# Neighbouring weight slabs of an expert kernel: one transfer of 8 KB rows for two of 4 KB

## The chip, the cores and the metric

The kernel runs on one core of one Trainium2 chip. The metric is device time in microseconds (us) of one execution. Engines are named as in the profile: PE (matrix multiply), DVE (vector), ACT (scalar), POOL (GpSimd), SP (the engine that issues most transfers). A transfer is carried out by 16 DMA engines that all queues share.

## The reference, cut to what matters

One block of a transformer: a projection, two attention branches with gates, an output projection with residual, and then a mixture of experts. The change lies in the last. Every token is weighted over its two chosen experts of 32:

```python
    weights = pg_sel * pe_top / jnp.sum(pe_top, axis=-1, keepdims=True)
    global_idx = g_idx * EXPERTS_PER_GROUP + e_idx
    combine = jnp.sum(jax.nn.one_hot(global_idx, N_EXPERTS, dtype=jnp.float32) * weights[..., None], axis=1)
    out = jnp.zeros((n, d), jnp.float32)
    for e in range(N_EXPERTS):
        hidden = jax.nn.silu(t @ w_gate[e]) * (t @ w_up[e])
        out = out + combine[:, e:e + 1] * (hidden @ w_down[e]).astype(jnp.float32)
```

There are 1024 tokens of 1024 values and 256 hidden values per expert; everything is float32.

## The kernel before, in words

The stages ahead of the experts (projection, attention, gates, output projection, router) take about 900 us of the span. The output projection runs over eight blocks of 128 tokens (`out_mm`, `x2_half`, `route`); weights for the experts are prefetched beside it.

**Weights.** The three matrices of an expert are laid out as one array `w_exp` of 128 partitions and 6144 values, and are read in six slabs of 128 x 1024 values, 512 KB each, 4 KB to a partition: 192 slabs for 32 experts, always in the same order (`raw_order`). A slab lands in a raw buffer. `weights(e, j0, j1)` then splits it into a high and a low part (`split`: ACT copies, rounding, L83; DVE subtracts, L84), and when that is done its buffer is free. Raw buffers come in units: five `er` and four `ex` (`N_RAW`, `N_MORE`) hold one slab each, and eight `ring` buffers hold two, side by side in a partition. When all slabs of a unit have been split, `weights` calls `load` for the next slabs in the order. `load_pairs` takes a new ring buffer. In `load`, each slab has a transfer of its own, on SP's queue. At the start 9 single slabs and 8 pairs are loaded; the pairs one after the other, as the output projection frees their buffers. As pairs are split in the expert stage, the first of them are not loaded again while at least `R_RAW` = 13 slabs are loaded or on their way: their buffers go to the gathers (`gbuf`, up to 9) and, after that, to the finished blocks (`ybuf`).

**One expert.** POOL gathers up to 112 rows of `h2_d` by token number (`gather`, L1111). PE transposes them (`tokens`, L1119), multiplies them with gate and up (`gate_up`), transposes the hidden values (`hidden_t`) and multiplies with down (`down`); each product is three matmuls (`mm3`, L87 to L89). In `down`, ACT writes the first half of the block, scaled by the tokens' weights, into a y buffer (L1160), DVE the second (L1162). POOL then scatters the block into `out`, adding to what is there (L1163). Scatters write the same array, so each waits for the one before it to have landed. A y buffer is used again when its scatter has landed.

**Order.** For PE, DVE and ACT the order around the router is that of the code; elsewhere a scheduler sets it at build time, from the code's order and from when buffers come free. SP's and POOL's queues run strictly in order. A transfer on SP's queue counts its landing in one of eight counters, taken in turn, and waits for the transfer that used the counter before it.

Of the kernel before, what the change touches and what calls it, by code (L numbers as in the profile page):

```python
# [10 lines left out]
F32 = mybir.dt.float32  # L11
# [13 lines left out]
P = 128  # L25
# [10 lines left out]
XTB = 4  # L36
NGB = 3
NYB = 3
N_MORE = 4
GB = 9  # L40
R_RAW = 13
LAGO = 1
# [6 lines left out]
def kernel(ctx: ExitStack, tc: tile.TileContext, a, out):  # L49
    nc = tc.nc  # L50
    left = dict(side="left", reuse_waits="tile")
# [30 lines left out]
    def split(hi, lo, src, eng=None):  # L82
        nc.scalar.activation(hi, src, AF.Copy)  # L83
        return (eng or nc.vector).tensor_tensor(lo, src, hi, op=ALU.subtract)  # L84
# [46 lines left out]
    def ring(dt):  # L131
        return pm.tile([P, 2, 1024], dt, name="ring", bufs=8)
# [5 lines left out]
    def er(i, dt=F32):  # L138
        return per.tile([P, 1024], dt, name=f"er{i % N_RAW}")
# [283 lines left out]
    for k in range(2):  # L423
        raw = er(next(raws))[:, :768]
        nc.sync.dma_start(raw, a["w_uq"][:, k, :])
        split(uqh[:, k, :], uql[:, k, :], raw)
    raw = er(next(raws))
# [256 lines left out]
    for n in range(MH * NT):  # L684
        h, i = divmod(n, NT)
# [56 lines left out]
    for m in range(DH * NT):  # L742
        h, i = divmod(m, NT)
# [43 lines left out]
    for b in range(KD):  # L787
        raw = er(b % 2)
# [30 lines left out]
    pex = ctx.enter_context(tc.tile_pool(name="pex", bufs=1, **right))  # L819
# [39 lines left out]
    RAW = {}  # L859
    raw_order = iter([(e, j) for e in range(NE) for j in range(6)])  # L860

    def load(unit):

        left = [len(unit)]
        for slab_ in unit:
            ej = next(raw_order, None)
            if ej is None:
                left[0] -= 1
                continue
            nc.sync.dma_start(slab_, a["w_exp"][ej[0], :, ej[1] * 1024:(ej[1] + 1) * 1024])  # L870
            RAW[ej] = (slab_, unit, left)

    def load_pairs(n):
        for _ in range(n):
            u = ring(F32)
            load([u[:, 0, :], u[:, 1, :]])

    X2, R2, XT2, RT, PS2, PL = {}, {}, {}, {}, {}, {}

# [137 lines left out]
    for t in range(2):  # L1017
        residual(t)
    for i in range(N_RAW):
        load([er(i)])  # L1020
    for i in range(N_MORE):
        load([pex.tile([P, 1024], F32, name=f"ex{i}")])
    with tc.manual_schedule(engines={mybir.EngineType.PE, mybir.EngineType.DVE, mybir.EngineType.Activation}):
        for t in range(NT):
            if 1 < t + 1 < NT:
                residual(t + 1)
            out_mm(t, 0, 0, 3)
            if t:
                x2_turn(t - 1, 0)
                x2_turn(t - 1, 1)  # L1030
                normed(t - 1)
            out_mm(t, 0, 3, KD)
            if t:
                logits(t - 1, 0, KD)
            x2_half(t, 0)
            out_mm(t, 1, 0, 6)
            if t:
                route(t - 1)
            weighted(t, 0)
            if t == NT - 1:  # L1040
                x2_turn(t, 0)
            out_mm(t, 1, 6, KD)
            if t:
                place(t - 1)
            x2_half(t, 1)
            if t % 2:
                load_pairs(2)
# [43 lines left out]
    def weights(e, j0, j1):  # L1091
        for j in range(j0, j1):
            raw, unit, left = RAW.pop((e, j))
            hi = pew.tile([P, 1024], F32R, name="ehi", bufs=7)
            lo = pew.tile([P, 1024], F32R, name="elo", bufs=7)
            split(hi, lo, raw)
            W[e, j] = (hi, lo)
            left[0] -= 1
            if left[0] or e == NE:
                continue  # L1100
            if len(unit) == 1:
                load(unit)
            elif len(RAW) < R_RAW:
                load_pairs(1)
            else:
                u = ring(F32)
                (gbuf if len(gbuf) + len(gused) < GB else ybuf).extend([u[:, 0, :], u[:, 1, :]])
# [72 lines left out]
    with tc.issue_after(acted.ins), tc.issue_after(listed.ins):  # L1180
        weights(0, 0, 6)
    tokens(0)
    for e in range(NE + 1):
        if e + 1 < NE:
            weights(e + 1, 0, 4)
# [5 lines left out]
        if e + 1 < NE:  # L1191
            weights(e + 1, 4, 6)
            turned = tokens(e + 1)
# [136 lines left out]
```

## Time and profile before

| what | value |
| --- | --- |
| median of 3 runs | 1274.68 us (1271.69 to 1276.09) |
| profiled execution, its own time | 1274.59 us |
| its span, first to last instruction | 1272.4 us |
| PE busy / DVE / ACT / POOL in the span | 1158.7 / 946.0 / 746.7 / 172.8 us |
| mean granted clock of PE | 0.966 |
| transfers of `w_exp` on SP's queue | 70 into er, 66 into ring, 56 into ex |

The page divides the span into 40 slices of 31.8 us; a digit is a busy share in tenths. The chain of waits is the work that ended last, followed backwards. A timeline lists instructions in order of time, with the idle time before each and what ended it in brackets; for a wait on several things the printed one may have been met long before.

### The profile page before, as it was taken

To read this page: it belongs to the slowest core of one execution; us is meant where nothing else is said; L and a number is where in the kernel's file an instruction comes from. 1 tells how busy PE (TensorE), PEld (TensorE's weight loads), DVE (VectorE), ACT (ScalarE), POOL (GpSimd) and SP (SyncE) were. 2 spreads that over 40 slices of the span, in tenths; PEclk is the share of its full clock that TensorE was granted. 3 is DMA by queue.
4 is the path that set the end of the run, shared out by engine and by line. 5 is a ranking of instruction groups with operands and counts; after the bars stand their busy time and mean duration, and the time that the engine had idled before them with its cause. 6 is when DMAs were issued, how large, how long until landed. Compare 5 with 4: busy or idle time off the path is not lost.

```text
span 1272.4 us, 18235 instructions
## 1 busy us (share of the span) xinstructions
PE 1158.7 (91%) x6105; PEld 946.7 (74%) x6105; DVE 946.0 (74%) x2099; ACT 746.7 (59%) x1400; POOL 172.8 (14%) x147
## 2 busy tenths in 40 slices
PE   7889999989999998999999999999399998788993
PEld 6778888868888886778777877888277766566772
DVE  4776783458888788888865775565599988778992
ACT  5544562356667677776663443323488877667881
POOL 1000000010000001111100000000155233423112
PEclk9989999999999999999999998999599999899997
DMA  8753475383232233431125446544769999999983
GB/s 254 230 176 108 116 195 161 101 181 94 81 92 75 75 112 88 116 116 51 66 95 195 141 140 254 184 166 156 235 209 338 298 316 319 311 301 332 355 302 51
DMA packets 107615, 228.62 MB, mean 180 GB/s; under 512 B 13984, under 2 KB 47392, under 8 KB 107520
## 3 DMA queue, kind: packets, MB, share of 16 engines
q1 hardware_dynamic: 81664, 193.59, 46.0%
q0 software_dynamic: 21248, 25.46, 9.7%
q10 hardware_dynamic: 4608, 8.39, 1.8%
q8 instruction: 49, 0.80, 0.3%
q14 instruction: 46, 0.38, 0.1%
HBM read 187.53 MB, written 52.43 MB: 189 GB/s over the span
## 4 chain that ended last, share of the span: by engine, by line
PE 47%; DMA 27%; DVE 12%; ACT 6%; issue 5%; POOL 1%; SPq 1%; POOLq 0%; ACTq 0%; DVEq 0%
PE pG L87 5%; PE pG L88 5%; PE pG L89 5%; DMA ring<-in_w_exp 5%; DMA ex<-in_w_exp 4%; DMA er<-in_w_exp 4%; PE pB L530 3%; DMA out<-ring,ids 3%; DMA sgl<-g_d 2%; PE pF L87 2%; PE pF L88 2%; PE pF L89 2%; PE pO L89 2%; DVE nbd L518 2%; PE pO L87 2%
## 5 line engine op out<-in xcount | busy, mean ns | idle before, releaser
L521 ACT ACTIVATE pd<-pA,nbd 128x512 f32<-128x512 f32 (+7 forms) x128 | 94.5, 739 | 39.1 <-DVE nbd L518 36.2
L87 PE MATMUL pG<-ring,whi 128*128 128x512 f32 x240 | 98.9, 412 | 4.8 <-ACT sg L495 4.7
L518 DVE TENSOR_REDUCE nbd<-pA 128x1 f32<-128x128 f32 (+7 forms) x128 | 95.7, 749 | 2.5 <-PE pA L569 1.5
L89 PE MATMUL pG<-ring,wlo 128*128 128x512 f32 x240 | 96.0, 400 | 0.0
L88 PE MATMUL pG<-ring,whi 128*128 128x512 f32 x240 | 95.7, 399 | 0.0
L84 DVE TENSOR_TENSOR elo<-er,ehi 128x1024 fp32r<-128x1024 f32 x70 | 82.9, 1221 | 8.6 <-ACT ehi L83 8.5
L84 DVE TENSOR_TENSOR elo<-ring,ehi 128x1024 fp32r<-128x1024 f32 x66 | 78.2, 1221 | 5.8 <-ACT ehi L83 5.8
L83 ACT ACTIVATE ehi<-er 128x1024 fp32r<-128x1024 f32 x70 | 72.4, 1057 | 16.5 <-DMA er<-in_w_exp 8.9
L83 ACT ACTIVATE ehi<-ring 128x1024 fp32r<-128x1024 f32 x66 | 69.0, 1059 | 17.1 <-PE pO L89 5.2
L84 DVE TENSOR_TENSOR elo<-ex,ehi 128x1024 fp32r<-128x1024 f32 x56 | 66.8, 1222 | 12.6 <-ACT ehi L83 12.4
L83 ACT ACTIVATE ehi<-ex 128x1024 fp32r<-128x1024 f32 x56 | 58.3, 1058 | 21.2 <-DMA ex<-in_w_exp 9.6
L87 PE MATMUL pG<-ehi,xh 128*112 128x512 f32 x128 | 53.2, 416 | 19.1 <-ACT xh L83 19.1
L530 PE MATMUL pB<-ident,pd 128*128 128x128 f32 x432 | 66.0, 277 | 1.9 <-DVE pd L573 0.9
L530 PEld LDWEIGHTS pB<-ident,pd 128*128 128x128 f32 x432 | 48.8, 141 | 12.5 <-PE pO L597 2.5
L89 PE MATMUL pB<-ehi,ehl 128*112 128x512 f32 x128 | 54.1, 423 | 3.4 <-DVE ehl L84 3.3
L87 PEld LDWEIGHTS pG<-ring,whi 128*128 128x128 f32 x240 | 45.6, 190 | 15.0 <-ACT sg L495 8.8
L87 PE MATMUL pB<-ehi,ehh 128*112 128x512 f32 x128 | 53.7, 420 | 0.7 <-DVE ring L1162 0.7
L1163 POOL DMA_INDIRECT out<-ring,ids x20 | 34.1, 1706 | 138.8 <-ACT esg L1134 45.0
L89 PEld LDWEIGHTS pG<-ring,wlo 128*128 128x128 f32 x240 | 45.8, 191 | 9.2 <-DVE wlo L84 0.2
L88 PE MATMUL pB<-elo,ehh 128*112 128x512 f32 x128 | 52.5, 410 | 0.0
L89 PE MATMUL pG<-ehi,xl 128*112 128x512 f32 x128 | 52.2, 408 | 0.0
L87 PE MATMUL pO<-ehi,xh 128*112 128x512 f32 x128 | 51.6, 403 | 0.6 <-ACT ehi L83 0.6
(395 smaller groups left out, 3574.9 us busy)
## 6 DMA issues: line engine op xcount, KB each, us to landing
er<-in_w_exp SPq DMA_DIRECT2D x70, 512.0 KB
ring<-in_w_exp SPq DMA_DIRECT2D x66, 512.0 KB
ex<-in_w_exp SPq DMA_DIRECT2D x56, 512.0 KB
er<-in_w_gate SPq DMA_DIRECT2D x16, 512.0 KB
g_d<-sg ACTq DMA_DIRECT2D x32, 256.0 KB
sgl<-g_d SPq DMA_DIRECT2D x32, 256.0 KB
er<-in_w_dqkv SPq DMA_DIRECT2D x8, 512.0 KB
xT<-in_xT SPq DMA_DIRECT2D x16, 256.0 KB
```

What stands on the lines that cost most here:

```text
L83: nc.scalar.activation(hi, src, AF.Copy)
L84: return (eng or nc.vector).tensor_tensor(lo, src, hi, op=ALU.subtract)
L87: nc.tensor.matmul(ps, ah, bh, start=start, stop=False)
L88: nc.tensor.matmul(ps, ah, bl, start=False, stop=False)
L89: nc.tensor.matmul(ps, al, bh, start=False, stop=stop)
L518: nc.vector.tensor_reduce(nb, ps[:, :n], axis=AX, op=ALU.max, negate=True)
L521: nc.scalar.activation(p[:, :n], ps[:, :n], AF.Exp, bias=nb, accum_out=s)
L530: nc.tensor.transpose(pt[:, (b - b0) * P:(b - b0 + 1) * P], p[:, b * P:(b + 1) * P], ident)
L1163: nc.gpsimd.indirect_dma_start(out=out[:, :], out_offset=bass.IndirectOffsetOnAxis(ap=idx[:BT, :], axis=0), in_=y[:BT, :], in_offset=None, ...
```

## The change

`load` now takes a unit as a pair: the whole buffer, as one access of 1024 or 2048 values to a partition, and the list of slabs in it. It draws as many slabs from the order as the unit holds, and reads them with one transfer, of 8 KB to a partition for a ring buffer. `N_MORE` falls from 4 to 3: with eight single slabs a pair always begins at an even slab, so both its slabs are of one expert. Nothing else is edited.

```diff
-N_MORE = 4
+N_MORE = 3
 GB = 9
 R_RAW = 13
...
-        left = [len(unit)]
-        for slab_ in unit:
-            ej = next(raw_order, None)
-            if ej is None:
-                left[0] -= 1
-                continue
-            nc.sync.dma_start(slab_, a["w_exp"][ej[0], :, ej[1] * 1024:(ej[1] + 1) * 1024])
+        left = [len(unit[1])]
+        ejs = [next(raw_order, None) for _ in unit[1]]
+        for ej, slab_ in zip(ejs, unit[1]):
             RAW[ej] = (slab_, unit, left)
+        e, j = ejs[0] or (None, None)
+        if e is None:
+            RAW.pop(None)
+            return
+        assert ejs[-1] == (e, j + len(ejs) - 1)
+        nc.sync.dma_start(unit[0], a["w_exp"][e, :, j * 1024:(j + len(ejs)) * 1024])
...
-            load([u[:, 0, :], u[:, 1, :]])
+            load((u.rearrange("p a n -> p (a n)"), [u[:, 0, :], u[:, 1, :]]))
...
-            if len(unit) == 1:
+            if len(unit[1]) == 1:
                 load(unit)
```

Of the 192 slabs, 88 come in 44 transfers of two and 104 in single ones.

In SP's queue, the place where rings are loaded again for the first time in the expert stage, before. `ring`, `er` and `ex` are raw buffers; `waits DMAHWn` is the wait for the transfer that used that counter before, `DVE` the wait for the split that frees the buffer:

```order
L870 DMA ex2_9005<-in_w_exp 128x1024 [waits DMAHW0_49,DVE_49]
L870 DMA ex3_9007<-in_w_exp 128x1024 [waits DMAHW1_49,DVE_49]
L870 DMA ring_10487<-in_w_exp 128x1024 [waits DMAHW2_49,DVE_49]
L870 DMA ring_10487<-in_w_exp 128x1024 [waits DMAHW3_49]
L870 DMA ring_10530<-in_w_exp 128x1024 [waits DMAHW4_49,DVE_49]
L870 DMA ring_10530<-in_w_exp 128x1024 [waits DMAHW5_49]
L870 DMA ring_10723<-in_w_exp 128x1024 [waits DMAHW6_49,DVE_49]
L870 DMA ring_10723<-in_w_exp 128x1024 [waits DMAHW7_49]
L870 DMA er0_8991<-in_w_exp 128x1024 [waits DMAHW0_49,DVE_49]
```

The same place on SP after the change:

```order
L873 DMA ex2_9005<-in_w_exp 128x1024 [waits DMAHW7_49,DVE_49]
L873 DMA ring_10424<-in_w_exp 128x2048 [waits DMAHW0_49,DVE_49]
L873 DMA ring_10434<-in_w_exp 128x2048 [waits DMAHW1_49,DVE_49]
L873 DMA ring_10483<-in_w_exp 128x2048 [waits DMAHW2_49,DVE_49]
L873 DMA ring_10663<-in_w_exp 128x2048 [waits DMAHW3_49,DVE_49]
L873 DMA er0_8991<-in_w_exp 128x1024 [waits DMAHW4_49,DVE_49]
```

Six transfers of three pairs before, and four transfers of four pairs now, stand between the second round of single slabs and the third; one counter is taken for each transfer, whatever its size.

In POOL's queue, the start of the expert stage before: gathers (L1111, out of `h2_d` into `g` and ring buffers) and the first scatters (L1163, out of y and ring buffers into `out`):

```order
L1111 DMA ring_10323<-h2_d_66,ids_10155 112x1024 x2
L1163 DMA out_0<-y0_10182,ids_10155 1024x1024
L1111 DMA g2_10178<-h2_d_66,ids_10155 112x1024
L1111 DMA g0_10176<-h2_d_66,ids_10155 112x1024
L1163 DMA out_0<-y1_10183,ids_10155 1024x1024
L1111 DMA ring_10292<-h2_d_66,ids_10155 112x1024 x2
L1163 DMA out_0<-y2_10184,ids_10155 1024x1024
L1163 DMA out_0<-ring_10389,ids_10155 1024x1024
```

The same place on POOL after the change:

```order
L1115 DMA ring_10314<-h2_d_66,ids_10145 112x1024 x2
L1115 DMA g2_10168<-h2_d_66,ids_10145 112x1024
L1167 DMA out_0<-y0_10172,ids_10145 1024x1024
L1115 DMA g0_10166<-h2_d_66,ids_10145 112x1024
L1167 DMA out_0<-y1_10173,ids_10145 1024x1024
L1115 DMA ring_10245<-h2_d_66,ids_10145 112x1024 x2
L1167 DMA out_0<-y2_10174,ids_10145 1024x1024
L1167 DMA out_0<-ring_10323,ids_10145 1024x1024
```

One gather, into `g2`, has moved from behind the first scatter to ahead of it. Further on, the scatters go round seven y buffers (three y, two rings of two) where they went round nine.

## Rows read from the trace of the kernel before

**Rows 1.** The page, whole span in 40 slices.

```profile
DMA  8753475383232233431125446544769999999983
```

**Rows 2.** Busy time by stretch: each engine (instructions), granted clock, DMA share, GB/s.

```profile
900.00:950.00 50.00, 36.96 (x176) 28.41 (x176) 34.80 (x35) 31.68 (x39) 22.49 (x14) 0.81 0.69 203
...
1000.00:1050.00 50.00, 47.54 (x227) 34.44 (x226) 43.87 (x48) 38.43 (x47) 16.95 (x11) 1.00 0.93 310
1050.00:1100.00 50.00, 41.14 (x192) 29.91 (x190) 38.82 (x41) 34.02 (x42) 17.56 (x9) 0.96 0.95 315
1100.00:1150.00 50.00, 41.84 (x184) 31.32 (x184) 38.04 (x41) 33.74 (x43) 19.38 (x10) 0.90 0.94 307
...
1200.00:1250.00 50.00, 49.13 (x235) 36.90 (x234) 45.08 (x50) 39.04 (x49) 10.44 (x6) 1.00 0.79 266
```

**Rows 3.** Chain of waits: start us, us, what.

```profile
1035.84 16.11 DMA ring<-in_w_exp
...
1130.29 17.98 DMA ex<-in_w_exp
...
1211.44 8.35 DMA out<-ring,ids
...
1253.89 5.54 DMA out<-ring,ids
```

**Rows 4.** Timeline of POOL: start us, us, instruction, idle before it.

```profile
954.02 8.50 POOL L1163 DMA_INDIRECT out<-y,ids  x1 [8.13 <-DVE y L1162]
...
970.87 1.51 POOL L1163 DMA_INDIRECT out<-y,ids  x1 [3.98 <-DVE cum L1209]
...
1156.89 6.10 POOL L1163 DMA_INDIRECT out<-y,ids  x1 [6.45 <-ACT ehi L83]
...
1240.40 2.36 POOL L1163 DMA_INDIRECT out<-y,ids  x1 [7.97 <-ACT ehi L83]
1247.64 1.46 POOL L1163 DMA_INDIRECT out<-y,ids  x1 [4.88 <-DMA out<-y,ids]
1253.89 1.46 POOL L1163 DMA_INDIRECT out<-ring,ids  x1 [4.79 <-ACTq L1217]
1260.22 1.46 POOL L1163 DMA_INDIRECT out<-ring,ids  x1 [4.88 <-DMA out<-ring,ids]
```

**Rows 5.** Timeline of DVE, second halves of finished blocks, columns as above.

```profile
953.23 0.75 DVE L1162 TENSOR_SCALAR y<-pB,wsl 112x512 f32<-112x512 f32 x1 [0.24 <-PE pB L89]
...
1155.20 0.75 DVE L1162 TENSOR_SCALAR y<-pB,wsl 112x512 f32<-112x512 f32 x1 [1.88 <-PE pB L89]
...
1254.09 0.75 DVE L1162 TENSOR_SCALAR ring<-pB,wsl 112x512 f32<-112x512 f32 x1 [2.89 <-PE pB L89]
```

**Rows 6.** DMA queues from 786 to 792 us: packets, MB, share of 16 engines.

```profile
DMA packets 683, 2.47 MB, mean 412 GB/s; under 512 B 80, under 2 KB 80, under 8 KB 683
...
q1 hardware_dynamic: 683, 2.47, 103.0%
```

**Rows 7.** DMA queues from 1228.5 to 1229 us.

```profile
q14 instruction: 1, 0.01, 3.9%
```

**Rows 8.** POOL's DMA queue, 1247.6 to 1253.8 and 1202 to 1211.4 us.

```profile
q0 software_dynamic: 128, 0.36, 37.8%
...
q0 software_dynamic: 128, 0.22, 12.2%
```

**Rows 9.** Waits of SP's queue, 900 to 1273: us in total, times, longest.

```profile
SPq L870 <- DMA er<-in_w_exp: 75.9, 49, 3.4
SPq L870 <- DMA ring<-in_w_exp: 63.8, 40, 4.0
...
SPq L870 <- DMA ex<-in_w_exp: 50.9, 39, 3.0
```

**Rows 10.** Timeline of SP's queue: issues, merged.

```profile
937.17 5.41 SPq L870 DMA_DIRECT2D ring<-in_w_exp  x6
...
1227.58 3.54 SPq L870 DMA_DIRECT2D ring<-in_w_exp  x2
```

More of the change, by code (lines that the diff above doesn't have):

```diff
@@ L1019 @@
     for i in range(N_RAW):
-        load([er(i)])
+        raw = er(i)
+        load((raw, [raw]))
     for i in range(N_MORE):
-        load([pex.tile([P, 1024], F32, name=f"ex{i}")])
+        raw = pex.tile([P, 1024], F32, name=f"ex{i}")
+        load((raw, [raw]))
     with tc.manual_schedule(engines={mybir.EngineType.PE, mybir.EngineType.DVE, mybir.EngineType.Activation}):
```

## The prediction

> **What bounds the kernel now.** I read the slices of the page first: the DMA engines are nearly full in the last quarter of the span alone, and that quarter is the expert stage, the only one that the change touches [rows 1]. There three things run close to their limits, so I looked for the one that sets the end. The table of stretches shows PE busy for 41 to 49 of every 50 us, the DMA engines at 0.93 to 0.95 from 1000 to 1150 us and at 0.79 from 1200 on, and the granted clock down to 0.90 where PE is hungry [rows 2]. The chain of waits goes from one weight transfer to the next between 1035.84 and 1148 us (seven pieces, first and last shown), and it ends on the scatters that add finished blocks into out [rows 3]. The timeline of POOL decides it. Every scatter waits for the one before, since both write out; the releaser printed beside it is a wait that had long been met. The block's second half was written at 953.23 us, and its scatter was issued at 970.87; at 1155.20 and 1156.89; at 1254.09 and 1260.22 [rows 4, 5]. So from the second scatter (954.02) on, a finished block was always there when the queue came free: **the end is the sum of the scatters' own times**, and PE and the weights matter only so far as they keep a block ready.
>
> Loaded and unloaded scatters differ. From 954.02 to 1240.40 there are 27 intervals, 286.4 / 27 = 10.6 us each; weights are then in flight (the last is issued about 1231). After that the intervals are 7.2, 6.3 and 6.3, 6.6 on average [rows 4, 10]. Landing alone took 8.35 us at 1211.44 and 5.54 at 1253.89 [rows 3]: 2.8 us of each loaded scatter is time that the weight traffic takes from it.
>
> **Part 1: rows of 8 KB.** 88 of the 192 slabs now come in 44 transfers, 104 stay single; 8 of the pairs are loaded before the stage, 36 in it. In a stretch with hardly anything but weights, 603 rows of 4 KB (683 packets less 80 small ones) took 1.030 x 16 x 6 = 98.9 us of engine time, 0.16 us a row, and 412 GB/s were moved [rows 6]. The trace has no weight row of 8 KB, but it has an 8 KB packet of the instruction queue: 3.9% of 16 x 0.5 us = 0.31 us [rows 7]. Two rows of 4 KB take 0.32 to 0.33 by the same view, so a pair saves 8 rows x 0.01 to 0.02 us on each engine, 0.1 to 0.16 us, and 36 pairs 3 to 6 us of a stage in which DMA is one of three limits. Bounds for the transfer rate are thus nothing and 4% on the pairs; I take 3 us. One landing instead of two makes the first half of a pair usable 512 KB / 412 GB/s = 1.3 us later, and the second no later; in a stretch that waits for weights that shifts the order, not the sum, so I charge 1 us once.
>
> The Trainium skill (DMA: Bandwidth & Descriptors) asks for at least 1 MiB a transfer (Rules for kernel authors) and fits a fixed cost of about 2.0 us to each (Anatomy of one DMA); by that 36 fewer transfers would be worth up to an estimated 72 us, and the kernel would end near 1203. The trace disagrees, so this gets no chance of its own: 512 KB transfers already ran at 412 GB/s back to back [rows 6], and a fixed cost lies under the transfers ahead.
>
> **Part 2: fewer transfers in flight counters.** Each transfer on SP's queue waits for the one eight before it (the order's DMAHW names). Those waits come to 75.9 + 63.8 + 50.9 = 190.6 us of SP's time in the stage [rows 9]. Eight transfers held 8 slabs; now 11 transfers carry 14 slabs, so eight hold 10.2. A deeper queue lets an engine that has few scatter rows run on while another lags. DMA shares of 0.93 to 0.95 in three stretches of 50 us [rows 2] bound this between 0 and 150 x 0.06 = 9 us; I take 2, since the buffers would soon limit instead.
>
> **Part 3: 14 slabs in the cycle for 13.** One single slab is gone, but the test on the number of raw slabs now hands over five ring pairs instead of six before it starts to reload them. The reload of rings, which began at 937.17 us, after 21 slabs were consumed [rows 10], begins after 18. DMA had slack there (a share of 0.69 from 900 to 950) [rows 2]. In a stretch bound by DMA this is worth the one more slab of capacity, 512 KB / 315 GB/s = 1.7 us. The pair that is not handed over is missing among the y buffers: 7 for 9. The lag between block and scatter was at most about 17 us, two intervals [rows 4, 5]; six outstanding blocks cover some 60, so this costs nothing, unless scatters fall that far behind. PE's, DVE's and ACT's orders keep their sequence but for single rows. On POOL one more gather goes ahead of the first scatter and one fewer behind it: what the first scatter loses the next gets back, 0.
>
> Sum for the weights: 3 + 2 + 1.7 - 1, about 6 us earlier; with scatters taking fewer turns from the weights (below) about 8.
>
> **Part 4: what longer rows do to the scatters.** A scatter is 128 packets, small and large, loaded or not [rows 8]: 16 engines x 8. If an engine takes a packet of the weights' queue and one of the scatter's in turn, 8 turns cost 8 x 0.16 = 1.3 us, which is about half of the 2.8 us; the rest lies ahead of its first packet. With 8 KB rows a turn costs 0.31: 8 x 0.15 = 1.2 us more while a pair is passing. A pair's rows take 8 x 0.31 = 2.5 us on an engine, a single's 1.3; three pairs are 7.4 of 17.7 us of a cycle, 42%. So 0.5 us more for a mean loaded scatter. Bounds: 0, if the engines share by bytes; 2.8 x 0.15 / 0.16 x 0.42 = 1.1 if all of the 2.8 us goes by packets. I take 0.5, the case between, because the 128 packets are the same number with and without load and only their spacing can have grown.
>
> **The sum.** Let weights end t earlier and a loaded interval be d longer. Loaded intervals then fit (286 - t) / (10.6 + d) times between 954 and 1240 - t, and the rest of the 30 up to the last issue run at 6.6. Before: 27, and 1240 + 3 x 6.6 = 1260 (it was 1260.2). With t = 8 and d = 0.5: 278 / 11.1 = 25.0, and 1232 + 5.0 x 6.6 = 1264.7, so **+4.5 us**. The block of the last expert, ready at 1254.09 before, is then ready by about 1246 and does not bind. The tail after the last issue, 12 us, stays. The profiled execution took 1274.59 us (span 1272.4), beside a median of 1274.68, so the forecast is 1279. Changes within 0.3% (3.8 us) are what a measurement of this kernel can't tell from none.
>
> **The rivals.**
> A (the forecast): turns by packet, start of a scatter unchanged. 1279.
> B: the engines share by bytes, or cut 8 KB rows anyway, so scatters stay as they are; weights 7 us earlier. 279 / 10.6 = 26.3 and 1233 + 3.7 x 6.6 = 1257.4: -2.9, 1272. That the transfer of 8 KB does nothing at all is its edge, 1274. For it: the bytes of the rows move at the same pace [rows 6].
> C, the slower side: what stands ahead of a scatter's first packet is also a number of packets, so that all of the 2.8 us grows; d is the upper bound, 1.1. 278 / 11.7 = 23.8, and 1232 + 6.2 x 6.6 = 1273: +13, 1288. Its place is the interval of each loaded scatter, and it decides from d of about 0.45 upward: there the loss passes 3.8 us. For it: the 8 turns explain only half of the 2.8 us. Against it: an engine can hold a bounded number of bytes as well as of packets.
> The Trainium skill (DMA: Bandwidth & Descriptors, Queues, rings and completion order) says that an engine changes between rings only at packet bounds and that such a packet spans several descriptors, typically 9 to 17. By that a scatter waits for whole transfers' shares of an engine, which pairs double; that speaks for C, and no row here shows which descriptors form a packet.
> D, faster: the deeper queue ends PE's hunger in 1050 to 1150, where PE was busy 83 of 100 us at clocks of 0.96 and 0.90 [rows 2]; weights end up to 25 us earlier with d = 0. 261 / 10.6 = 24.6 and 1215 + 5.4 x 6.6 = 1250.6: -9.6, 1265. Against it: DMA is already 0.93 to 0.95 full there.
>
> **How the numbers follow.** A 0.38, B 0.30, C 0.17, D 0.15. A lies at the bound of 3.8 us, 0.25 of it beyond and 0.13 inside; B is inside with 0.21 and beyond it on the fast side with 0.09. Faster 0.24, same 0.34, slower 0.42. The range takes in A, B and most of C and D, with 1266 to 1292; A's own range is 1274 to 1284.
>
> **What would show it.** A's first step: weight rows of 8 KB at about 0.31 us each, and a rate in pure stretches hardly above 412 GB/s. The second: loaded scatter intervals of about 11.1 us where they were 10.6, with every scatter still issued on the landing of the one before. The third: the last weight issued near 1223, and some five unloaded scatters at the end in place of three. B would show intervals of 10.6, C of 11.7, D PE at over 47 of 50 us between 1050 and 1150. I am wrong altogether if a scatter waits for its block over a long stretch, or if the lag grows past 60 us, so that 7 buffers hold PE up.

## The result and the profile after

The changed kernel took 1286.66 us (median of five runs, 1286.03 to 1292.32) beside 1274.68 for the kernel before (five runs, 1270.99 to 1277.46). The ratio is 1.0105, with a 95% interval of 1.0077 to 1.0133: about 12 us slower, where 4.5 were forecast. The profiled execution took 1286.43 us, its span 1284.7, so that the extra time of the span (12.3 us) is the extra time of the median.

The page's slices of the whole span, after, to be laid beside [rows 1]: the expert stage again fills the DMA engines, and its end has become longer by a slice that is half empty.

```profile
DMA  7844474463323243342044437654599999899943
```

Busy time by stretch of 50 us, after (us; PE, PEld, DVE, ACT, POOL with instructions; granted clock; DMA share; GB/s), for [rows 2]:

```profile
1000.00:1050.00 50.00, 46.16 (x226) 34.94 (x225) 45.22 (x49) 39.17 (x50) 25.01 (x10) 0.98 0.97 338
1050.00:1100.00 50.00, 42.59 (x202) 31.65 (x202) 40.73 (x44) 36.10 (x45) 12.76 (x10) 0.99 0.92 305
1100.00:1150.00 50.00, 39.99 (x180) 29.51 (x179) 36.06 (x40) 31.14 (x39) 14.23 (x8) 0.93 0.91 299
...
1200.00:1250.00 50.00, 48.81 (x235) 36.79 (x234) 44.73 (x51) 38.00 (x48) 9.27 (x6) 1.00 0.66 223
```

Between 1050 and 1150 PE is busy for 82.6 of 100 us, where it was 83.0, and the DMA engines move no more than before. The weights are not the place where the time went.

POOL's timeline after (start us, us, instruction, idle before it), for [rows 4]: the second scatter, the last ones beside the weights, and those that run alone.

```profile
951.20 7.02 POOL L1167 DMA_INDIRECT out<-y,ids  x1 [10.87 <-ACT ehi L83]
...
1230.74 1.46 POOL L1167 DMA_INDIRECT out<-ring,ids  x1 [9.47 <-ACT y L1164]
1240.43 1.82 POOL L1167 DMA_INDIRECT out<-ring,ids  x1 [8.23 <-DVE ehd L1140]
1247.06 1.46 POOL L1167 DMA_INDIRECT out<-ring,ids  x1 [4.80 <-DMA out<-ring,ids]
...
1272.32 1.46 POOL L1167 DMA_INDIRECT out<-ring,ids  x1 [4.79 <-DMA out<-y,ids]
```

Here the whole loss can be counted. From 951.20 to 1240.43 there are 25 intervals, 289.2 / 25 = **11.57 us each; before they took 10.6**. At the same moment, 1240.4 us, the kernel before had three scatters left to issue behind that one, and the changed one has five. They run at 31.9 / 5 = 6.4 us each, so two more cost 12.8 us, and the last issue moved from 1260.22 to 1272.32, by 12.1.

The chain of waits after, its last pieces (start us, us, what), for [rows 3]. It enters the scatters at 1230.74 and stays on them to the end:

```profile
1230.74 8.90 DMA out<-ring,ids
...
1253.21 5.81 DMA out<-y,ids
```

DVE's second halves of blocks, after, for [rows 5]:

```profile
1204.04 0.75 DVE L1166 TENSOR_SCALAR ring<-pB,wsl 112x512 f32<-112x512 f32 x1
...
1252.00 0.75 DVE L1166 TENSOR_SCALAR ring<-pB,wsl 112x512 f32<-112x512 f32 x1 [2.90 <-PE pB L89]
```

The block of 1204.04 is scattered at 1230.74, and the last one, of 1252.00, at 1272.32: these two lay ready for 26 and 20 us. All 32 scatters were issued after their blocks had been written, so none waits for PE, which finished 2 us earlier than before (1254.09).

SP's queue after, its last issues, for [rows 10], and the DMA queues in two stretches, for [rows 6]: 934 to 936 us, where little but weight rows of 8 KB pass, and the loaded stage, 950 to 1231 us.

```profile
1210.04 5.56 SPq L873 DMA_DIRECT2D ex<-in_w_exp  x3
1218.39 2.93 SPq L873 DMA_DIRECT2D ring<-in_w_exp  x3
```

```profile
DMA packets 109, 0.82 MB, mean 412 GB/s; under 512 B 8, under 2 KB 8, under 8 KB 9
...
q1 hardware_dynamic: 107, 0.82, 101.1%
```

```profile
DMA packets 22568, 89.92 MB, mean 320 GB/s; under 512 B 4706, under 2 KB 4706, under 8 KB 18502
```

In the short stretch 100 rows of 8 KB took 1.011 x 16 x 2 = 32.4 us of engine time: 0.32 us a row, twice the 0.16 of a 4 KB row, at the same 412 GB/s. In the loaded stage 320 GB/s were moved; the kernel before moved 91.34 MB between 954 and 1240 us, 319 GB/s. Longer rows bring nothing to the rate of this kernel.

### The profile page after: what moved, and what is told of

The parts are those of the page before. It is cut to its first block, busy times and chain, and to the rows that moved or that the text cites. A ratio compares the mean times of both kernels' runs of the same rounds, so it can differ in the third digit from the quotient of the medians.

```text
span 1284.7 us, 18141 instructions
## 1 busy us (share of the span) xinstructions
PE 1155.6 (90%) x6105; PEld 945.7 (74%) x6105; DVE 946.3 (74%) x2099; ACT 745.9 (58%) x1400; POOL 177.8 (14%) x147
## 4 chain that ended last, share of the span: by engine, by line
PE 49%; DMA 25%; DVE 12%; ACT 7%; issue 5%; POOL 1%; SPq 1%; POOLq 0%; ACTq 0%; DVEq 0%
DMA ring<-in_w_exp 7%; PE pG L87 6%; PE pG L88 5%; PE pG L89 5%; DMA ex<-in_w_exp 3%; PE pB L530 3%; DMA er<-in_w_exp 2%; DMA sgl<-g_d 2%; PE pO L89 2%; PE pO L87 2%; PE pO L88 2%; PE pF L87 2%; PE pF L88 2%; PE pB L89 2%; PE pF L89 2%
## 5 line engine op out<-in xcount | busy, mean ns | idle before, releaser
L84 DVE TENSOR_TENSOR elo<-ring,ehi 128x1024 fp32r<-128x1024 f32 x88 | 104.4, 1220 | 20.6 <-ACT ehi L83 20.6
L83 ACT ACTIVATE ehi<-ring 128x1024 fp32r<-128x1024 f32 x88 | 91.8, 1058 | 35.3 <-DMA ring<-in_w_exp 21.6
L84 DVE TENSOR_TENSOR elo<-er,ehi 128x1024 fp32r<-128x1024 f32 x65 | 77.0, 1220 | 4.7 <-ACT ehi L83 4.5
L83 ACT ACTIVATE ehi<-er 128x1024 fp32r<-128x1024 f32 x65 | 67.1, 1056 | 13.0 <-DMA er<-in_w_exp 4.5
L1167 POOL DMA_INDIRECT out<-ring,ids x17 | 39.0, 2297 | 126.8 <-DVE elo L84 25.4
L666 PE MATMUL pA<-x,x 128*128 128x512 f32 (+3 forms) x168 | 47.9, 370 | 3.8 <-ACT pd L521 3.7
L88 PE MATMUL pG<-elo,xh 128*112 128x512 f32 x128 | 51.1, 400 | 0.0
```

The costliest lines, as they stand in the source:

```text
L88: nc.tensor.matmul(ps, ah, bl, start=False, stop=False)
L666: nc.tensor.matmul(ps[f][:, k], q, ks[f][j][:, k], start=j == 0, stop=j == 1)
L1167: nc.gpsimd.indirect_dma_start(out=out[:, :], out_offset=bass.IndirectOffsetOnAxis(ap=idx[:BT, :], axis=0), in_=y[:BT, :], in_offset=None, ...
```

## Experiments

Theory T: a loaded scatter takes longer because its rows wait their turn behind rows of 8 KB. Rivals: other parts of the change (order, 14 slabs, fewer y buffers), the size or number of the transfers, the start of a scatter, the gathers. "Loaded interval" below is the time from the second scatter's issue to the 26th's, over 24 (before 10.73, after 11.65). It comes from one profiled execution of each kernel; the four kernels with rows of 4 KB and the old layout of tokens lie between 10.65 and 10.92. Each ratio is against the kernel before on the same chip.

### Pairs again as two transfers of 4 KB rows

```diff
-        nc.sync.dma_start(unit[0], a["w_exp"][e, :, j * 1024:(j + len(ejs)) * 1024])
+        for i, slab_ in enumerate(unit[1]):
+            nc.sync.dma_start(slab_, a["w_exp"][e, :, (j + i) * 1024:(j + i + 1) * 1024])
```

> The changed kernel, but each pair comes with two transfers of 4 KB rows again; 14 slabs in the cycle, 7 y buffers and the order of buffers stay as the change has them. Theory (the length of the rows sets the scatters' times): loaded scatter intervals back to 10.6 to 10.8 us, time 1272 to 1277. Rival 1 (what slows it is the rest: 14 slabs for 13, 7 y buffers for 9, another order on the queues): 1284 to 1290. Rival 2 (it is the number of bytes in flight, 10 slabs' worth in eight transfers): also 1272 to 1277, so this run alone does not tell it from the theory.

Ratio 1.0007 (0.9976 to 1.0038). POOL's timeline of this kernel, second and 26th scatter:

```profile
958.59 1.51 POOL L1168 DMA_INDIRECT out<-y,ids  x1 [8.49 <-DVE xl L84]
...
1215.85 1.92 POOL L1168 DMA_INDIRECT out<-ring,ids  x1 [7.78 <-ACT esg L1139]
```

257.3 / 24 = 10.72 us, the interval of before. The eight single slabs, the 14 in the cycle, the order and the buffers cost nothing and gain nothing that can be measured. The loss lies in the one transfer.

### One transfer for two slabs, with rows of 4 KB

The two halves of a ring buffer are set 16 bytes apart, so a pair is one transfer of 1 MB whose rows are 4 KB.

```diff
-        return pm.tile([P, 2, 1024], dt, name="ring", bufs=8)
+        return pm.tile([P, 2, 1028], dt, name="ring", bufs=8)[:, :, :1024]
...
+        src = a["w_exp"][e, :, j * 1024:(j + len(ejs)) * 1024]
+        if len(ejs) == 2:
+            src = src.rearrange("p (a n) -> p a n", a=2)
+        nc.sync.dma_start(unit[0], src)
```

> The changed kernel with one transfer of 1 MB for a pair, but rows of 4 KB: the two halves of a ring buffer stand 16 bytes apart in SBUF, so that a row ends at each slab. Number of transfers, order and bytes in flight as in the change. Theory (row length): 1270 to 1277, loaded intervals 10.6 to 10.8 us. Rival 2 (bytes in flight, fewer and larger transfers): 1284 to 1290.

Ratio 1.0004 (0.9985 to 1.0023); loaded interval 10.92 us (958.19 to 1220.24). So it is the row's length, not the number or the size of the transfers or the bytes in flight. This kernel differs from the changed one in the rows alone: by it their price is 11.65 - 10.92 = 0.73 us an interval, and 0.92 by the kernel before. This run also settles what larger transfers are worth here: nothing. The Trainium skill (DMA: Bandwidth & Descriptors, Rules for kernel authors) wants 1 MiB or more to a transfer; with transfers that follow each other without a gap, this run shows no gain from it.

### Two transfers for two slabs, with rows of 8 KB

Each of them takes 64 partitions.

```diff
+        for h in range(2):
+            nc.sync.dma_start(unit[0][h * 64:(h + 1) * 64, :],
+                              a["w_exp"][e, h * 64:(h + 1) * 64, j * 1024:(j + 2) * 1024])
```

> The changed kernel with two transfers for a pair, each of 64 partitions with rows of 8 KB: rows as in the change, number of transfers and bytes in eight transfers as before it. Theory (row length): 1284 to 1291, loaded intervals about 11.6 us. Rival 2 (bytes in flight): 1272 to 1277.

A miss of another kind: ratio 1.1017 (1.098 to 1.1054). Busy time by stretch, columns as above:

```profile
1050.00:1100.00 50.00, 40.77 (x174) 28.96 (x174) 30.34 (x35) 26.90 (x34) 9.92 (x6) 0.92 1.00 213
1100.00:1150.00 50.00, 33.45 (x123) 22.77 (x122) 27.11 (x27) 22.66 (x27) 9.70 (x7) 0.83 1.00 208
```

The DMA engines count as fully busy and move 208 to 213 GB/s in place of some 310. Transfers over half the partitions made the weights the bound, and PE starves. This run says nothing on the theory; it says that transfers over 64 partitions were a bad trade here.

### Nine y buffers again

One more pair is handed over to the y buffers, which leaves 12 slabs in the cycle.

```diff
-R_RAW = 13
+R_RAW = 12
```

> The changed kernel with R_RAW = 12, so that six pairs are handed over as before the change: 12 slabs in the cycle instead of 14, and 9 y buffers instead of 7; two pairs in it instead of three. Theory (row length): 8 KB rows then carry 4 of 12 slabs instead of 6 of 14, a share of 33% against 42%, so a quarter of the loss goes: 1282 to 1287. Rival 1 (7 y buffers hold PE up): 1274 to 1278.

Ratio 1.012 (1.0071 to 1.017), loaded interval 11.72 us (964.27 to 1245.51). The y buffers are not the cause. Whether the loss goes with the pairs' share can't be read from the ratio: within an interval of half a per cent to each side a quarter of 12 us is hard to see. The interval divides, though, into POOL's own time for the scatter's instruction and the rest, up to the next one's issue. The first happened to be longer in this run, 2.73 us for 2.48 in the changed kernel. The rest is 8.99 us here, 9.17 in the changed kernel, and 8.34 on average in the four kernels with 4 KB rows: +0.65 for +0.83, where the expected shares of 8 KB rows are 33% for 42%. That agrees with a proportion, as far as single executions go.

### The price by itself: scatters beside rows of 2 to 24 KB

Only scatters, each waiting for the one before, and whole experts of 3 MB that come in rows of one length after another.

```diff
+    for r_ in (512, 1024, 2048, 3072, 6144):
+        k_ = 6144 // r_
+        for _ in range(20):
+            w_ = cst.tile([P, 48 * (128 + 4)], F32, name="w", bufs=4)
+            w_ = w_[:, :k_ * (r_ + 4)].rearrange("p (k n) -> p k n", n=r_ + 4)[:, :, :r_]
+            nc.sync.dma_start(w_, a["w_exp"][n_ % NE].rearrange("p (k n) -> p k n", n=r_))
```

> The disputed cost by itself, nothing of the block is computed: x is written to out, then POOL scatters 96 blocks of 112 rows into out one after the other (64 rows valid, zeros are added, as many rows as a mean expert has), while SP's queue loads whole experts of 3 MB one after the other, 20 each with rows of 2, 4, 8, 12 and 24 KB (the destination has a gap after every row). Bytes in flight are the same throughout. Theory (an engine takes packets of the two queues in turn, the start of a scatter does not change): the interval grows by 8 x 0.15 = 1.2 us from 4 to 8 KB, by 2.4 to 12 KB, by 6 to 24 KB, and shrinks by 0.6 from 4 to 2 KB. Rival B (engines share by bytes): the same interval for all rows. Rival C (start too goes by packets): from 4 to 8 KB 2.6 us more. After the loads the interval is 6.2 to 6.3 us.

POOL's timeline, first and last scatter of the stretches with 4 KB (21 intervals), 8 KB (17) and 24 KB (11), and of the one without weights (7):

```profile
225.38 1.46 POOL L68 DMA_INDIRECT out<-y,ids  x1 [7.29 <-DMA out<-y,ids]
...
413.36 1.46 POOL L68 DMA_INDIRECT out<-y,ids  x1 [7.31 <-DMA out<-y,ids]
...
432.24 1.46 POOL L68 DMA_INDIRECT out<-y,ids  x1 [8.40 <-DMA out<-y,ids]
...
601.89 1.46 POOL L68 DMA_INDIRECT out<-y,ids  x1 [8.82 <-DMA out<-y,ids]
...
817.06 1.46 POOL L68 DMA_INDIRECT out<-y,ids  x1 [12.42 <-DMA out<-y,ids]
...
973.84 1.46 POOL L68 DMA_INDIRECT out<-y,ids  x1 [12.18 <-DMA out<-y,ids]
982.56 1.46 POOL L68 DMA_INDIRECT out<-y,ids  x1 [7.27 <-DMA out<-y,ids]
...
1024.55 1.46 POOL L68 DMA_INDIRECT out<-y,ids  x1 [4.58 <-DMA out<-y,ids]
```

| weight rows | none | 2 KB | 4 KB | 8 KB | 12 KB | 24 KB |
| --- | --- | --- | --- | --- | --- | --- |
| interval, us | 6.0 | 8.4 | 8.95 | 9.98 | 11.2 | 14.25 |

The rise is nearly even, 0.25 to 0.31 us for each KB of row. From 4 to 8 KB it is 1.03 us; a row takes 0.15 to 0.16 us longer, so that is about 7 turns, and 112 rows on 16 engines are 7 to an engine. That is the theory's mechanism and nearly its 8 turns. The trace's packet records agree: beside rows of 8 KB, a row of the weights starts 0.02 us before the end of each of the 1088 scatter rows with data. Drawn back to rows of no length (8.4 less 2 x 0.28) some 7.8 us remain, 1.8 more than without weights: a part of the cost that the row's length doesn't touch. The records agree: a scatter's first row with data starts 2.0 us after its issue without weights, and 4.2, 4.1, 4.8, 4.0 and 4.3 us beside rows of 2, 4, 8, 12 and 24 KB. Had all of the extra time gone by rows, 8 KB would have cost 6.0 + 2 x 2.95 = 11.9 us. The Trainium skill (DMA: Bandwidth & Descriptors, Queues, rings and completion order) has the engines change between rings at packet bounds, with several descriptors to a packet. The first agrees with this table; a turn of nine descriptors would have cost 7 x 9 x 0.15, over 9 us, where the table has 1.03, so here a turn is one row.

### Rows of 2 KB, and a control

The kernel before, with `w_exp` laid out in host memory as blocks of 128 x 512, so that all weight rows are 2 KB; and the control, blocks of 128 x 1024 with rows of 4 KB as before.

```diff
+            nc.sync.dma_start(slab_.rearrange("p (a n) -> p a n", n=512),
+                              a["w_exp"][ej[0], 2 * ej[1]:2 * (ej[1] + 1)].rearrange("a p n -> p a n"))
```

> The kernel before, with rows of 2 KB for all weight slabs: the weights lie in HBM in blocks of 128 x 512, so that one transfer of 512 KB reads two blocks. Transfers, order and buffers as before. Theory (row length, turns by packet): loaded scatter intervals 0.5 us shorter, 10.1 to 10.3; but rows of 2 KB move at some 5% less, so DMA, which is nearly full, ends its weights 5 to 10 us later, PE ends later, and the time is within 0.3% of before or up to 0.7% above. Rival B (share by bytes): intervals of 10.6 us and 0.3 to 1% above.

> Comparison for the run with 2 KB rows: the kernel before with the weights in HBM in blocks of 128 x 1024, rows of 4 KB as before, so that only where the rows stand in HBM differs. All theories: within 0.3% of before, loaded intervals 10.6 to 10.8 us.

The 2 KB kernel has a ratio of 1.0024 (1.0001 to 1.0047), the control of 0.9977 (0.9957 to 0.9998) with a loaded interval of 10.65 us. Shorter rows make no faster kernel. The loaded interval of the 2 KB kernel is 10.97 us: neither the 10.1 to 10.3 that the theory asked for nor the rival's 10.6. DVE's and POOL's timelines show a part of the reason: a block's second half, and the scatter that takes it.

```profile
1090.60 0.75 DVE L1163 TENSOR_SCALAR y<-pB,wsl 112x512 f32<-112x512 f32 x1 [2.75 <-PE pB L89]
```

```profile
1092.15 5.13 POOL L1164 DMA_INDIRECT out<-y,ids  x1 [7.38 <-ACT ehi L83]
```

This block was finished at 1091.35, 0.80 us before its scatter, and five more scatters are issued 0.77 to 0.80 us after their blocks, where the kernel before has one below 2.4 us (0.94, at 1156.89). At six places, then, the scatters had caught up with the blocks, and the chain waited for PE. How much of the missing gain these waits took, the run doesn't show. It does show that rows below 4 KB had nothing to give to this kernel.

### Do gathers add to it?

The sweep with two gathers after every second scatter, rows of 2 to 12 KB, nothing of the block computed.

```diff
+        if _ % 2:
+            for i in range(2):
+                nc.gpsimd.indirect_dma_start(
+                    out=g_[:BT, :], out_offset=None, in_=a["x"][:, :],
```

> The sweep of row lengths once more (nothing of the block is computed), 88 scatters, rows of 2, 4, 8 and 12 KB, and after every second scatter two gathers of 112 rows on POOL's queue, as in the expert stage. In the sweep without them the interval grew by 1.0 us from 4 to 8 KB, and the start did not move. Theory 1 (gathers' packets take turns too, and those that are not through when the next scatter is issued stand ahead of it): the mean interval grows by 1.4 to 2.2 us from 4 to 8 KB, more in the intervals that follow gathers; 42% of that is the 0.9 us that the changed kernel showed. Theory 2 (gathers don't matter, the kernel's 0.9 us come from elsewhere): again 1.0 us.

POOL's timeline, a stretch beside 4 KB rows (20 intervals) and one beside 8 KB rows (17):

```profile
375.39 1.45 POOL L68 DMA_INDIRECT out<-y,ids  x1 [7.78 <-DMA out<-y,ids]
...
554.28 1.45 POOL L68 DMA_INDIRECT out<-y,ids  x1 [7.42 <-DMA out<-y,ids]
...
573.02 1.45 POOL L68 DMA_INDIRECT out<-y,ids  x1 [8.41 <-DMA out<-y,ids]
...
743.30 1.45 POOL L68 DMA_INDIRECT out<-y,ids  x1 [8.67 <-DMA out<-y,ids]
```

178.9 / 20 = 8.94 and 170.3 / 17 = 10.02 us: the step is 1.07, as in the sweep before. But these stretches hold no gathers. The scheduler had put them elsewhere: those behind the first scatter are all issued between 166 and 310 us, beside rows of 2 KB, and the last of them at 308.46. There 16 intervals took 8.74 us each, with 8.4 in the sweep without gathers. What gathers do beside 4 and 8 KB rows was thus not measured, and the rival stands.

The kernels' own traces bear on it. POOL's timeline of the changed kernel shows two gathers (L1115) queued ahead of a scatter, and the DMA issues from 950 to 1231 us the median time from a gather's issue to its landing:

```profile
1119.33 1.03 POOL L1115 DMA_INDIRECT ring<-h_d,ids  x1 [0.30 <-issue]
1120.66 1.00 POOL L1115 DMA_INDIRECT ring<-h_d,ids  x1 [0.30 <-PE pB L89]
1129.15 1.63 POOL L1167 DMA_INDIRECT out<-y,ids  x1 [7.49 <-ACT esg L1138]
1141.36 1.49 POOL L1167 DMA_INDIRECT out<-ring,ids  x1 [10.57 <-DVE elo L84]
```

```profile
ring<-h_d,ids POOLq DMA_INDIRECT x13, 13.7
g<-h_d,ids POOLq DMA_INDIRECT x6, 11.5
```

The scatter of 1129.15 is issued 8.5 us after the second gather, which lands at 1137.2, so rows of gathers are still on their way. Divided by this, the 25 intervals from the second scatter on are:

| kernel | weight rows | 11 scatters right behind gathers, us | 14 others, us |
| --- | --- | --- | --- |
| before | 4 KB | 11.31 | 10.16 |
| two transfers of 4 KB rows | 4 KB | 11.37 | 10.14 |
| one transfer, 4 KB rows | 4 KB | 11.36 | 10.46 |
| blocks of 128 x 1024 | 4 KB | 10.92 | 10.40 |
| after | 8 KB, mixed | 12.72 | 10.67 |
| nine y buffers | 8 KB, mixed | 12.61 | 10.93 |

From before to after, the 14 others became 0.51 us longer, and the 11 behind gathers 1.41. This points to the gathers: their rows stand ahead of the scatter in POOL's queue, and would take turns with the longer rows as well. It is read from single executions, and no run takes the gathers away.

### Does the mix of short and long rows add to it?

The stretches come in this order: 126 single slabs; nine times three pairs with 8 KB rows and eight singles; 63 pairs with 8 KB rows; 63 transfers of 1 MB with 4 KB rows ("b").

```diff
+CYCLES = (("1", 126), ("22211111111", 9), ("2", 63), ("b", 63))
```

> The scatters alone again, the block's computation left out, beside weight transfers as the kernels issue them, in four stretches: 512 KB with 4 KB rows; the mix of the changed kernel, three 1 MB transfers of 8 KB rows and then eight of 512 KB with 4 KB rows, over and over; 1 MB with 8 KB rows only; 1 MB with 4 KB rows only. Theory 'turns': a scatter costs what the mean row beside it costs, so the mixed stretch lies 42% of the way from the first to the third, about 9.4 us where these are near 8.95 and 9.95, and the fourth equals the first. Theory 'mix': a scatter ends with its slowest engine, and where long and short rows alternate some engine is always in long ones; then the mixed stretch is at 9.85 or more, about as far from the first as the pure 8 KB stretch, which would give the changed kernel's 0.9 us. A third case, the length of the transfer and not of the row, would show the fourth stretch above the first.

POOL's timeline: the mixed stretch's first scatter, three in its middle and its last (23 intervals), then the stretch with 8 KB rows alone (first and last scatter, 18 intervals):

```profile
233.22 1.46 POOL L67 DMA_INDIRECT out<-y,ids  x1 [7.25 <-DMA out<-y,ids]
...
260.82 1.46 POOL L67 DMA_INDIRECT out<-y,ids  x1 [7.22 <-DMA out<-y,ids]
270.73 1.46 POOL L67 DMA_INDIRECT out<-y,ids  x1 [8.45 <-DMA out<-y,ids]
279.55 1.46 POOL L67 DMA_INDIRECT out<-y,ids  x1 [7.37 <-DMA out<-y,ids]
...
445.39 1.46 POOL L67 DMA_INDIRECT out<-y,ids  x1 [7.22 <-DMA out<-y,ids]
...
455.15 1.46 POOL L67 DMA_INDIRECT out<-y,ids  x1 [8.29 <-DMA out<-y,ids]
...
631.44 1.46 POOL L67 DMA_INDIRECT out<-y,ids  x1 [8.15 <-DMA out<-y,ids]
```

Intervals: 8.74 us beside 512 KB transfers of 4 KB rows (58.63 to 215.95, 18 intervals), 9.22 in the mix, 9.79 beside 8 KB rows alone, 8.85 beside 1 MB transfers of 4 KB rows (659.96 to 757.29, 11). The mix lies 0.48 / 1.05 = 46% of the way, close to the 43% (6 of 14 slabs) that "turns" asks for; "mix" falls. One sees how it comes about: a scatter in the mix waits either about 7.3 us or about 8.4, as its rows met a burst of singles or of pairs. And a larger transfer alone costs 0.1 us. This run also shows what the rows are worth to the rate where only weights and scatters pass: 354 GB/s in all with 8 KB rows alone, 345 and 341 with 4 KB rows.

### Valid rows spread over the partitions

From the sweeps and [rows 8] another lever came up. In a block of 112 rows only those with a token are scattered, and they sit in neighbouring partitions. Here the list of slots is laid out with a stride of 7, so that an expert's tokens lie spread; done to the kernel before, to the changed kernel, and to the control with blocks of 128 x 1024.

```diff
+    nc.gpsimd.iota(slotp[:, :BT].rearrange("p (a b) -> p a b", b=7), pattern=[[1, 16], [16, 7]], base=0,
+                   channel_multiplier=0, allow_small_or_imprecise_dtypes=True)
...
-            nc.vector.tensor_scalar(sl, slots, pc_, None, op0=ALU.is_equal)
+            nc.vector.tensor_scalar(sl, slotp, pc_, None, op0=ALU.is_equal)
```

> The kernel before, with the order of an expert's tokens over the 112 partitions changed: token j goes to partition (j mod 16) x 7 + j / 16, so that the 64 valid rows of a mean scatter fall on all 16 engines, 4 each, instead of on 64 neighbouring partitions, up to 7 on an engine. Weights as before, 4 KB. Theory (the scatters' chain sets the end, and the engine with the most rows sets a scatter): loaded intervals 0.5 to 1 us shorter, unloaded ones 6.3 to about 5.5, time 0.3 to 1% less, then bound by PE and the weights. If PE and the weights bound it already: within 0.3%.

> The changed kernel (8 KB rows) with the tokens spread over the partitions in the same way. Theory: the rows of 8 KB still cost each scatter its turns (8 for each engine, empty ones too), 0.5 to 0.9 us, so it stays slower than the spread kernel with 4 KB rows by about what the change cost, 0.5 to 1%, or less where PE binds by then: 0.997 to 1.005 of the kernel before. If row length costs only through engines full of valid rows: equal to the spread kernel with 4 KB rows.

> A version meant to beat both kernels: weights in HBM in blocks of 128 x 1024 (which gave 0.998 of before) and tokens spread over the partitions; 4 KB rows. Theory: what the spread kernel with 4 KB rows gains, and 0 to 0.3% more.

| kernel | median us | ratio to before | 95% interval |
| --- | --- | --- | --- |
| before, spread | 1246.47 | 0.978 | 0.975 to 0.981 |
| after, spread | 1253.97 | 0.9823 | 0.9787 to 0.9859 |
| blocks of 128 x 1024, spread | 1249.07 | 0.9783 | 0.9752 to 0.9814 |

All three beat both kernels, by more than was expected (0.3 to 1% for the first, 0.997 to 1.005 for the second); the best is **the kernel before with spread tokens**, 2.2% faster. Its stretches, and its last scatters:

```profile
1050.00:1100.00 50.00, 49.34 (x245) 37.47 (x243) 48.79 (x54) 42.80 (x54) 17.60 (x12) 1.00 1.04 368
1100.00:1150.00 50.00, 49.29 (x236) 37.26 (x235) 48.45 (x54) 41.60 (x52) 14.49 (x9) 1.00 1.03 367
```

```profile
946.91 1.52 POOL L1168 DMA_INDIRECT out<-y,ids  x1 [6.56 <-DVE jc L1219]
...
1211.20 2.31 POOL L1168 DMA_INDIRECT out<-y,ids  x1 [4.00 <-DVE y L1167]
...
1230.33 1.46 POOL L1168 DMA_INDIRECT out<-ring,ids  x1 [4.64 <-DMA out<-ring,ids]
```

```profile
1199.44 0.75 DVE L1167 TENSOR_SCALAR y<-pB,wsl 112x512 f32<-112x512 f32 x1 [0.34 <-PE pB L89]
...
1219.97 0.75 DVE L1167 TENSOR_SCALAR ring<-pB,wsl 112x512 f32<-112x512 f32 x1 [2.89 <-PE pB L89]
```

The DMA engines move 367 GB/s where they moved 307 to 315 [rows 2], and PE is busy 49 of 50 us at a granted clock of 1.00. The scatters still set the end: the block scattered at 1211.20 had been finished at 1200.19, the last one at 1220.72, 9.6 us before its scatter, and none was issued less than 6.7 us after its block. DVE's name beside 1211.20 is a wait that had been met. What became shorter is the loaded interval: the 27 from 946.91 to 1211.20 took 9.79 us each, where 27 took 10.6, some 22 of the 30 us by which the last issue moved (1260.22 to 1230.33). The second scatter, 7 us earlier, gave most of the rest. The three intervals that run alone did not shrink to the expected 5.5 us: 6.85, 6.18 and 6.10.

A likely reading of the higher rate is that the scatters and gathers had kept a part of the 16 engines busier than the rest, and each weight slab landed with its slowest engine; the profile doesn't show the engines one by one, so this is argued. With spread tokens 8 KB rows still cost 0.4%, 0.9823 / 0.978 = 1.004; the two intervals overlap. Divided as above, that cost too lies behind the gathers: 9.93 and 9.91 us (behind gathers, others) with 4 KB rows, 10.97 and 9.67 with 8 KB rows, in single executions again. The layout in blocks adds nothing.

## Why the prediction was right, and where it was off

**What bounds the kernel: right.** The end is the sum of the scatters. No scatter of the changed kernel waited for a block, and the loss is two scatters more that had to run behind the weights. In the kernel before, one was close: the block for 1156.89 was done 0.94 us ahead.

**Rival A's course: right in kind.** Its own range, 1274 to 1284, was missed by 3 us. Loaded intervals grew, and five scatters ran alone at the end in place of three, as put down. The last weight was issued at 1221.3 (forecast near 1223). Rows of 8 KB took 0.32 us (0.31), at 412 GB/s (hardly above 412). B is out, since the interval did grow; D is out with PE at 82.6 of 100 us.

**Part 1, 8 KB rows save 3 us: not in this kernel.** The price came from one 8 KB packet of another queue. It was about right for the weights' own rows: where only they and scatters pass, the engines moved 354 GB/s with 8 KB rows and 341 to 345 with 4 KB rows. But in the expert stage the rate was 320 for 319, the lower bound given, nothing. That the kernel with one transfer of 4 KB rows is not faster than before (1.0004) says the same of **part 2** (2 us) and **part 3** (1.7 us): neither showed. The last weight was issued 10 us earlier. A part of that reached the landings: the rate falls sooner after than before (after first, columns as above):

```profile
1230.00:1235.00 5.00, 5.00 (x25) 3.74 (x24) 4.63 (x6) 4.91 (x6) 1.46 (x1) 1.00 0.41 125
```

```profile
1230.00:1235.00 5.00, 5.00 (x23) 3.71 (x24) 4.64 (x7) 4.03 (x5) 1.46 (x1) 1.00 0.88 321
```

The last weight row ended at 1238.1 us, 4.5 us earlier than before. The scatters got nothing of it: in both kernels the one issued at 1240.4 is the first that runs free. The sum's t of 8 us was thus 4.5 for the weights, about 0 for the scatters, and 2 us for PE's last block.

**Part 3, y buffers: right.** The longest lag grew from 17 us to 32 (a block written at 1097.53 was scattered at 1129.15), under the 60 that seven buffers cover, and nine of them changed nothing.

**Part 4, the mechanism right, the size half.** d was 11.57 - 10.6 = 0.96 us and not 0.5; it lay between the bounds, 0 and 1.1, near the upper one. The sum's own formula gives 286.4 / 11.57 = 24.75 and 1240.4 + 5.25 x 6.6 = 1275.0 for this d with t at 0, which is +14.8; the 2.8 us by which the second scatter came earlier (951.20 for 954.02) bring that to the measured +12.1. By the same formula the mis-sized d alone is worth 7 us (t of 8: +11.2) and the mis-sized t alone 3.4 (d of 0.5: +7.9). The estimate's own pieces held: about 7 turns for 8, 1.03 to 1.05 us beside 8 KB rows alone for 1.2, and a mix that pays by its share, 0.48 for 0.5. But all of that is measured with scatters and weights alone.

**In the kernel the same mix costs 0.73 to 0.96, and what adds the rest is not shown.** Not its cause: the order and the slabs of the change, the size or number of the transfers, the y buffers, the alternation of short and long rows. Nor do the scatters meet the pairs more often than their share: in the last 4.3 us before a landing 39% of the weights' bytes came in 8 KB rows, with 42% over the stage. The traces point to the gathers. The scatters that are not behind gathers became 0.51 us longer, just what part 4 put down for all; the 11 behind gathers became 1.41 us longer. Part 4 counted only a scatter's own rows. Two gathers ahead of it are 14 more rows to an engine, by estimate up to 14 x 0.15 x 0.42 = 0.9 us, for those of them that are still on their way.

**Rival C: near in size, its mechanism wrong for scatters alone.** Its 1288 was nearer to 1286.66 than the forecast's 1279. In the sweep a scatter's start does not grow with the row: the 1.8 us that length doesn't touch is there at every length. In the kernel, though, rows of gathers stand ahead of 11 of the 25 scatters, and if these pay by the row, C's mechanism is at work there. The range (1266 to 1292) held the time because C's size had been left in it, with a chance of 0.17; that was caution and not a reading.

## What to carry to other kernels

When several queues share the DMA engines, a longer row for the bulk traffic is a longer turn for every small row beside it: look for a serial chain of small transfers before lengthening the rows of a large one, and price it as rows per engine times the growth of a row's time. That gave the whole price for a chain that has its queue to itself, and about half of it in the kernel, where gathers stood in the same queue: count the rows queued ahead of each link too. Count how many links of such a chain are still to come when the traffic ends, since the loss shows up there and not at the link that became longer. And look at how the rows of a scatter or gather fall on the partitions: spreading them was worth more here than any row length that was tried.

## What the runs showed of the hardware beyond that

- The kernel with its pairs cut into two transfers over 64 partitions moved 205 to 216 GB/s at a DMA share of 0.96 to 1.00, where the changed kernel, with the same rows in one transfer over 128, moved 299 to 338; it was 10% slower than the kernel before.
- Beside weight traffic a scatter of 112 rows took about 1.8 us longer at any row length (its first row with data started 2.0 to 2.8 us later), and 0.25 to 0.31 us more for each KB of the traffic's rows.
- With valid rows spread over the partitions the same bytes moved at 343 to 373 GB/s between 1000 and 1200 us, against 307 to 341, and the granted clock stayed at 1.00, where it had fallen to 0.90 while PE waited for weights.
